# Opening the first layer of a two-layer decoder trunk from packed, feature-major inputs

## The chip, the cores and the metric

The kernel runs on one core of one Trainium2 chip. The metric is the device time of one execution in microseconds (us); before the change it is 2598.28 us, the median of three runs (2598.2 to 2599.01).

## What is computed

A trunk of two layers on 1024 tokens with 1024 features. Each layer normalises the tokens, projects them, runs two attention mixers (a dilated windowed one and a "stick-breaking" one), merges them through gates, adds the result to the residual stream `x`, and then runs a gated convolutional feed-forward part with 2816 channels. What matters here is the very beginning of layer 0:

```
def rmsnorm(x, g):
    y = x * rsqrt(mean(x * x, axis=-1) + 1e-6)
    return y * g

h = rmsnorm(x, norm1[l])
proj = h @ w_in[l]
qa, ka, va, qb, kb, vb, gate_pre = split(proj, ...)
z = qb @ kb.T / 8                        # stick-breaking scores, per head
later = reversed running sum of log(1 - sigmoid(z)) over earlier keys
o_b = exp(log(sigmoid(z)) + later) @ vb
```

A token's norm factor multiplies its whole row of `h`, so `vb` can be formed from `x * g` first and be multiplied by the token's factor afterwards.

## The kernel before

Activations stand feature-major on chip: 128 partitions hold features, the free dimension holds tokens, 8 feature chunks `k`, two token halves `n` of 512. Products on TensorE (PE) use float32 data split in two parts: `hi`, a rounded copy made by ScalarE (ACT), and `lo = x - hi`, made by VectorE (DVE). Each product is three matmuls (`product`, L187 to L189): hi by hi, hi by lo, lo by hi. So every operand costs one ACT and one DVE instruction on 128x512.

Layer 0 begins with `first` and `head`. `first` loads `x` token-major, eight tiles of 128 tokens (`xr`, L2023), squares each on ACT with an accumulated row sum (L2053), takes the root and reciprocal (L2056, L2057), and turns the tiles on PE (`x_t`, L2044; 64 transposes of `x` itself and 16 of the two tiles that are scaled before they are turned, `xsq`). ACT copies the turned tiles out of PSUM (`x_part`, L2073), from where they are stored to `xs` in DRAM for the residual stream, and DVE scales them with the gain and the factor (`h_raw`, L2090). `head` makes 256 value columns (`v_ps`, four banks of 48 matmuls of 256 columns), then keys and queries of the first two stick-breaking heads (`kq_ps`, `q_ps`, 24 matmuls of 512 columns for each of the two token halves). Part of the weight splitting and the rebuilding of `h_raw` for the first tokens runs on GpSimd (POOL; L175, L176, L2037, L2110).

Behind the opening comes the dense stage. It takes column pairs of `w_in` (`pair`, tile `in_a`) through a scheme of seven half-size products instead of eight (`seven`, L1058 to L1060, tiles `i_a`, `i_b`, `i_c`). The scheme needs sums of quarters of `h`: `block_sums` makes `h_sum` (L1081, L1086), rewrites `h_raw` in place (L1087, L1090), and splits the sums into `t_hi`, `t_lo`; and sums of quarters of the weights, L1186, L1189, L1193, each followed by a split into `w_hi`, `w_lo` (L145, L153). All of this is DVE and ACT work. Between these products stands the stick-breaking attention: scores `z` (L648, L649), sigmoids on ACT (`beta`, `stay`), a running product on DVE (L743), `beta * stay` on DVE (L750), and a transposition of that on PE (`sb_t`, L758).

PE's order is the program's order throughout. ACT and DVE run their queues in order too; what stands where in them is set by the program's order in the first steps (`manual_schedule`) and by the scheduler of the framework after that. All DMAs that matter are issued by SyncE (SP) in order, over eight semaphores in turn.

Of the kernel before, what the change touches and what calls it, by code (L numbers as in the profile page):

```python
# [34 lines left out]
WARM = 3  # L35
# [22 lines left out]
TWICE = 2  # L58
# [7 lines left out]
def trunk_kernel(ctx, tc, x, norm1, vecs, w_in, w_br, w_o, w_up, w_down, norm_f, out, depth=None, probe=None):  # L66
# [12 lines left out]
    make_identity(nc, ident)  # L79
    ones = cp.tile([P, 1], F32, name="ones")  # L80
    pool.memset(ones, 1.0)
    eps = cp.tile([P, 1], F32, name="eps")
    pool.memset(eps, EPS)
    zero = cp.tile([P, 1], F32, name="zero")
    pool.memset(zero, 0.0)
# [6 lines left out]
    def masks():  # L92

        t = [sb.tile([P, 256], F32, tag="pt", bufs=PT, name=f"msk{i}") for i in range(3)]
        pool.iota(t[1], [[-1, 256]], base=P, channel_multiplier=1, allow_small_or_imprecise_dtypes=True)
        pool.affine_select(t[1], t[1], [[-1, 256]], ALU.is_ge, FAR, base=P, channel_multiplier=1)
        pool.affine_select(t[2], t[1], [[1, 256]], ALU.is_ge, FAR, base=0, channel_multiplier=-1)
        dve.tensor_copy(base0, t[2])
        pool.memset(over, 0.0)
        pool.affine_select(over[:, HF - P : HF], over[:, HF - P : HF], [[-1, P]], ALU.is_gt, 1.0, base=0, channel_multiplier=1)  # L100
        rem = sb.tile([P, 256], I32, tag="pt", bufs=PT, name="rem")
        pool.iota(rem, [[-1, 256]], base=256, channel_multiplier=1)
        one = dve.tensor_scalar(rem, rem, 3, None, ALU.bitwise_and)
        tc.add_manual_dep(one.ins, LAST["g0"], NO_SYNC, reason="in turn")
        dve.tensor_copy(t[0], rem)
        dve.tensor_scalar(t[0], t[0], FAR, None, ALU.mult)
        LAST["base"] = dve.tensor_tensor(base2, t[1], t[0], ALU.add).ins.name

# [52 lines left out]
    def weights(src, cols, place=None, eng=None):  # L161
# [3 lines left out]
        src = src.rearrange("(k p) n -> p k n", p=P)  # L165
        for r in range(0, KD, per):
# [7 lines left out]
            if eng:  # L174
                eng.tensor_copy(hi, raw)  # L175
                LAST.setdefault("pools", []).append(pool.tensor_tensor(lo, raw, f32(hi), ALU.subtract).ins.name)  # L176
            else:
                split(hi, lo, raw)
# [286 lines left out]
    def x_in(n, h):  # L465

        if h == 0:
            X[n] = [None, None]
        X[n][h] = quarter(f"x{n}")
        nc.sync.dma_start(X[n][h], xs[n][:, 4 * h : 4 * h + 4, :])  # L470
# [137 lines left out]
    def kq_half(c, w, n):  # L608
        o = bank("ps", "kq_ps"[c:])
# [7 lines left out]
    def head(l, dense=None):  # L617


        def place(n, name):  # L620
            x = [big(name, F32R) for _ in range(n)]
            return ([x[0][:, h, :] for h in range(2)] if n == 1 else [y.rearrange("p a b -> p (a b)") for y in x])

        wv = weights(w_in[l][:, OFF_VB : OFF_VB + 256], 256, place(2, "v_w")) if l else early.pop("wv")
        others = lambda: [weights(w_in[l][:, off : off + P], P, place(1, "kq_w"), None if l else pool) for off in (OFF_KB, OFF_QB)]
        if l:
            wk, wq = others()
        yield
        vt = new_v("vb")
        if l:  # L630
            yield from values_part(vt, wv, range(2))
        else:
            yield from values_part(vt, wv, range(1))
            wk, wq = others()
            yield from values_part(vt, wv, range(1, 2))
        for n in range(2):
            yield from kq_half(0, wk, n)
            yield from kq_half(1, wq, n)
            if n == 0 and not l:
                one = table(AF.Sigmoid, zero[:, 0:1])  # L640
                tc.add_manual_dep(one.ins, LAST["head"][0], NO_SYNC, reason="behind")
                yield from values_part(vt, wv, range(2, 4))
                dense.done.add("wv")
        if l:
            yield from values_part(vt, wv, range(2, 4))
# [685 lines left out]
    def mixer(l, pending):  # L1331
# [19 lines left out]
        else:  # L1351
            first_units = relay(head(l, dense))

            with tc.manual_schedule(engines={ET.Activation, ET.DVE}):
                next(pending)
                next(first_units)
                for n in (1, 2):
                    next(pending)
                    for _ in range(n):
                        next(first_units)  # L1360
            for i, _ in enumerate(pending):
                for _ in range(2):
                    next(first_units, None)
                if i == 3:
                    dense.prime(1)
            for _ in first_units:
                dense.aside()
# [85 lines left out]
        for i, ab in order:  # L1453
            n, e = todo[i]
            sl = slice(n * HF, (n + 1) * HF)
            if i not in seen:
# [4 lines left out]
                if i in X_AT:  # L1461
                    late_x = X_AT.index(i)
                    x_in(late_x // 2, late_x % 2)
# [436 lines left out]
    heads, early = {}, {}  # L1900
# [109 lines left out]
    def first():  # L2010
        g_raw = sb.tile([KD, P], F32, tag="ot", name="g_raw")
        nc.scalar.dma_start(g_raw, norm1[0].rearrange("(c p) -> c p", p=P))
        gb = [bank("o", "gb") for _ in range(2)]
        warm = sb.tile([P, 8], F32, tag="ss", bufs=2, name="warm")
        act.activation(warm[:, 0:1], eps, AF.Sqrt)
        xr, rest, tps, parts, factor, raw_t, part = {}, {}, {}, {}, {}, {}, {}
        raw = big("w_raw").rearrange("p a (b c) -> p (a b) c", c=256)
        wv = early["wv"] = []

        def load(i):  # L2020
            if i < 8:
                xr[i] = sb.tile([P, T], F32, tag="p4", bufs=4, name="xr")
                nc.sync.dma_start(xr[i], xin[i * P : (i + 1) * P, :])  # L2023

        def weights_in(r):
            nc.sync.dma_start(raw[:, r : r + 2, :], w_in[0].rearrange("(k p) n -> p k n", p=P)[:, r : r + 2, OFF_VB : OFF_VB + 256])

        def weights_hi(r):
            hi = sb.tile([P, 2, 256], F32R, tag="wh", bufs=4, name="w_hi")
            lo = sb.tile([P, 2, 256], F32R, tag="wl", bufs=4, name="w_lo")  # L2030
            act.copy(hi, raw[:, r : r + 2, :])
            wv.extend((hi[:, i, :], lo[:, i, :]) for i in range(2))
            parts[r] = hi, lo

        def weights_lo(r, eng=dve):
            hi, lo = parts[r]
            one = eng.tensor_tensor(lo, raw[:, r : r + 2, :], f32(hi), ALU.subtract)  # L2037
            if eng is pool:
                LAST["pool"] = one.ins.name

        def turned(src, tag):
            got = [bank(tag, "x_t") for _ in range(2)]
            for k in range(KD):
                pe.transpose(got[k // 4][:, (k % 4) * P : (k % 4 + 1) * P], src[:, k * P : (k + 1) * P], ident)  # L2044
            return [tp.rearrange("p (e t) -> p e t", e=4) for tp in got]

        def scaled(i):
            if i in (0, 2):
                rest["pair"] = big("xsq")
            sq = rest[i] = rest["pair"][:, i % 2, :] if i < 4 else sb.tile([P, T], F32, tag="ot", name="xsq")  # L2050
            ss = factor[i] = sb.tile([P, 8], F32, tag="ss", bufs=2, name="ss")
            with tc.high_priority(offset=AHEAD):
                one = act.activation(sq, xr[i], AF.Square, accum_out=ss[:, 0:1])  # L2053
                if i >= TWICE + 2:
# [175 lines left out]
```

## Time and profile before

| | |
|---|---|
| median of three runs | 2598.28 us |
| the profiled execution | 2600.39 us, of which the span of its instructions is 2598.4 us |
| PE busy | 99% of the span, granted clock 0.999 |
| DVE, ACT, POOL busy | 80%, 52%, 4% |
| first product of `v_ps` | 9.12 us from the span's start |
| first product of the dense stage (`i_a`) | 65.02 us |
| first `sb_t` transposition | 82.63 us |

Times in rows are from the span's start. In a timeline row the first number is the start, the second the time from there to the end of the last instruction of the row; instructions of one kind that follow each other are one row (`x4`), and what ended a wait stands in brackets. Since instructions on one engine overlap a little, the distance of two starts is the price of one instruction; the time of a row with n of them, less one duration, over n-1 gives it too.

### The profile page before, as it was taken

The numbers are of one execution on the slowest core, as the hardware profiler recorded it, in microseconds if no ns is written. First come the engines' busy times: TensorE is split into PE (matmuls) and PEld (weight loads), VectorE is DVE, ScalarE is ACT, GpSimd is POOL, SyncE is SP. The second block draws the span as 40 slices with busy tenths as digits, with TensorE's granted clock in tenths as the row PEclk, the third lists the DMA queues.
The fourth block names the chain that finished last, engine by engine and source line by source line (L and its number), as shares of the span: only waits on it lengthen the run. The fifth ranks groups of instructions, "written<-read, shape, count | busy, mean of one in ns | idle before, by whom it ended". The sixth has DMA issues, their size and how long they took to land.

```text
span 2598.4 us, 35940 instructions
## 1 busy us (share of the span) xinstructions
PE 2585.0 (99%) x12600; PEld 2161.4 (83%) x12600; DVE 2088.0 (80%) x3482; ACT 1340.1 (52%) x2506; POOL 105.5 (4%) x145
## 2 busy tenths in 40 slices
PE   9999999999999999999999999999999999999999
PEld 8888888888888888888888888888888888888887
DVE  8878777795988888897678788777869888889966
ACT  6555666573554555422445565666645555544223
POOL 3000000030000000000000000000300000000000
PEclk9999999999999999999999999999999999999999
DMA  7534588973344444688444446798633344456963
GB/s 256 153 119 134 161 209 225 236 237 97 90 146 157 143 163 146 235 327 315 152 143 148 126 132 175 199 238 239 205 99 121 125 154 154 140 176 246 346 242 134
DMA packets 400772, 470.59 MB, mean 181 GB/s; under 512 B 24616, under 2 KB 315856, under 8 KB 398800
## 3 DMA queue, kind: packets, MB, share of 16 engines
q1 hardware_dynamic: 399728, 465.90, 56.1%
q0 software_dynamic: 704, 2.13, 0.4%
q8 instruction: 100, 1.64, 0.3%
q14 instruction: 80, 0.66, 0.1%
q10 hardware_dynamic: 160, 0.27, 0.0%
HBM read 305.59 MB, written 162.63 MB: 180 GB/s over the span
## 4 chain that ended last, share of the span: by engine, by line
PE 92%; DVE 4%; ACT 2%; DMA 1%; issue 1%; POOL 0%; DVEq 0%; ACTq 0%; POOLq 0%
PE u_a L1058 5%; PE u_a L1059 5%; PE u_a L1060 5%; PE d_ps L1818 5%; PE d_ps L1819 5%; PE d_ps L1820 5%; PE i_a L1058 5%; PE i_a L1059 5%; PE i_a L1060 5%; PE u_c L1058 3%; PE u_c L1059 3%; PE u_c L1060 3%; PE i_c L1058 2%; PE i_c L1060 2%; PE i_c L1059 2%; PE o_ps L188 2%
## 5 line engine op out<-in xcount | busy, mean ns | idle before, releaser
L145 ACT CAST w_hi<-up_a 128x512 fp32r<-128x512 f32 x280 | 173.9, 622 | 277.2 <-DVE up_a L1672 120.8
L153 DVE TENSOR_TENSOR w_lo<-up_a,w_hi 128x512 fp32r<-128x512 f32 x280 | 189.5, 689 | 83.5 <-ACT w_hi L145 83.5
L145 ACT CAST w_hi<-in_a 128x512 fp32r<-128x512 f32 x252 | 156.3, 622 | 161.6 <-PE i_c L1059 33.2
L153 DVE TENSOR_TENSOR w_lo<-in_a,w_hi 128x512 fp32r<-128x512 f32 x252 | 172.8, 688 | 72.6 <-ACT w_hi L145 60.6
L1829 DVE TENSOR_TENSOR x<-x,d_ps 128x512 f32<-128x512 f32 x220 | 150.2, 684 | 60.5 <-PE d_ps L1820 57.2
L1058 PE MATMUL u_a<-hh,w_hi 128*128 128x512 f32 x320 | 124.5, 389 | 0.0
L1060 PE MATMUL u_a<-hh,w_lo 128*128 128x512 f32 x320 | 124.5, 389 | 0.0
L1059 PE MATMUL u_a<-t_lo,w_hi 128*128 128x512 f32 x320 | 124.5, 389 | 0.0
L1060 PE MATMUL u_a<-t_hi,w_lo 128*128 128x512 f32 x320 | 124.5, 389 | 0.0
L1059 PE MATMUL u_a<-hl,w_hi 128*128 128x512 f32 x320 | 124.5, 389 | 0.0
L1058 PE MATMUL u_a<-t_hi,w_hi 128*128 128x512 f32 x320 | 124.5, 389 | 0.0
L1818 PE MATMUL d_ps<-gd_in,w_hi 128*128 128x512 f32 x316 | 123.2, 390 | 0.0
L1819 PE MATMUL d_ps<-gd_in,w_hi 128*128 128x512 f32 x316 | 123.0, 389 | 0.0
L1820 PE MATMUL d_ps<-gd_in,w_lo 128*128 128x512 f32 x316 | 123.0, 389 | 0.0
L1058 PE MATMUL i_a<-hh,w_hi 128*128 128x512 f32 x288 | 117.8, 409 | 0.0
L1058 PE MATMUL i_a<-t_hi,w_hi 128*128 128x512 f32 x288 | 116.5, 404 | 0.0
L1060 PE MATMUL i_a<-hh,w_lo 128*128 128x512 f32 x288 | 113.1, 393 | 0.0
L1060 PE MATMUL i_a<-t_hi,w_lo 128*128 128x512 f32 x288 | 113.0, 392 | 0.0
L1059 PE MATMUL i_a<-t_lo,w_hi 128*128 128x512 f32 x288 | 113.0, 392 | 0.0
L1059 PE MATMUL i_a<-hl,w_hi 128*128 128x512 f32 x288 | 112.9, 392 | 0.0
L1818 PE MATMUL d_ps<-gd_in,wd 128*128 128x512 f32 x284 | 110.9, 390 | 0.0
L1820 PE MATMUL d_ps<-gd_in,wd 128*128 128x512 f32 x284 | 110.5, 389 | 0.0
(403 smaller groups left out, 7723.4 us busy)
## 6 DMA issues: line engine op xcount, KB each, us to landing
gd<-g SPq DMA_DIRECT2D x154, 512.0 KB, 3.1
gd_in<-gd SPq DMA_DIRECT2D x154, 512.0 KB, 6.0
up_a<-in_w_up_dram SPq DMA_DIRECT2D x80, 512.0 KB, 5.4
in_a<-in_w_in_dram SPq DMA_DIRECT2D x72, 512.0 KB, 5.4
wd_raw<-in_w_down_dram SPq DMA_DIRECT2D x22, 1024.0 KB, 10.9
gin<-gs SPq DMA_DIRECT2D x32, 512.0 KB, 4.5
w_raw<-in_w_o_dram SPq DMA_DIRECT2D x64, 256.0 KB, 3.0
gs<-u SPq DMA_DIRECT2D x48, 256.0 KB, 3.2
```

The lines of the kernel that those rows point to most:

```text
L145: one = act.copy(hi, src)
L153: two = dve.tensor_tensor(lo, src, f32(hi), ALU.subtract)
L188: pe.matmul(o, lh, rl, start=False, stop=False, skip_group_check=share)
L1058: pe.matmul(o, w[0][:, c], rh, start=(first and i == 0), stop=False, skip_group_check=True)
L1059: pe.matmul(o, w[0][:, c], rl, start=False, stop=False, skip_group_check=True)
L1060: pe.matmul(o, w[1][:, c], rh, start=False, stop=(last and i == 3), skip_group_check=True)
L1818: pe.matmul(o, wh[:, c], gh, start=(i == 0 and k in (0, 4, 5)), stop=False, skip_group_check=True)
L1819: pe.matmul(o, wh[:, c], gl, start=False, stop=False, skip_group_check=True)
L1820: pe.matmul(o, wl[:, c], gh, start=False, stop=(i == m - 1), skip_group_check=True)
L1829: dve.tensor_tensor(x, x, o, ALU.add)
```

## The change

The host hands in three packed arrays more: `xt`, the transposed `x` in three blocks of tokens (0 to 255, 256 to 511, 512 to 1023); `wh`, the columns of `w_in` for values, keys and queries of the head, laid out by partition; and `gt0`, the first gain by partition. The opening becomes one function:

- `x` comes feature-major into the tiles `h_raw` by DMA, 256 tokens and two chunks at a time, alternating with value weights. The 80 transposes, the copies out of PSUM, the store to `xs` and all GpSimd work on weights and `h_raw` are gone.
- For tokens 0 to 511, ACT and DVE make `hi` and `lo` of `x * g` (L2040, L2044, 128x256 each), PE makes the value products from those, and the factor is applied when the bank is read out (L2139, L2137).
- The sums of squares come from ACT squares (L2048), DVE additions and 16 matmuls with a column of ones (L2085), followed by root, reciprocal and four transposes that spread the factors (`nrm_b`, L2119).
- DVE then multiplies `h_raw` in place by gain and factor (L2124), and ACT and DVE split it again (L2125, L2128), for keys and queries: chunk by chunk, PE following (L2148 to L2150). Key and query weights are split by ACT and DVE (L2104, L2108).
- The second 512 tokens are scaled likewise; their squares are taken token-major on ACT (L2178) from four tiles of `x` loaded beside. PE makes their values (L2058), then their keys and queries.
- The residual `x` is read from `xt` instead of `xs`; layer 1's head reads its weights from `wh`.

The core of the diff:

```diff
-            first_units = relay(head(l, dense))
-            with tc.manual_schedule(engines={ET.Activation, ET.DVE}):
-                next(pending)
-                next(first_units)
...
+            opening = first(dense)
+            with tc.manual_schedule(engines={ET.Activation, ET.DVE, ET.Pool}):
+                next(opening)
+            for _ in opening:
                 dense.aside()
...
+        def u_hi(k, t):
+            act.mul(H[0][0][:, k, t], RAW[0, k // 4][:, k % 4, t], g0[:, k : k + 1])
+        def u_lo(k, t):
+            hi, lo = (y[:, k, t] for y in H[0])
+            dve.scalar_tensor_tensor(lo, RAW[0, k // 4][:, k % 4, t], g0[:, k : k + 1], f32(hi), ALU.mult, ALU.subtract)
...
+        def scale(n, k, rb):
+            h_ = RAW[n, k // 4][:, k % 4, :]
+            dve.scalar_tensor_tensor(h_, h_, g0[:, k : k + 1], rb, ALU.mult, ALU.mult)
+            act.copy(H[n][0][:, k, :], h_)
+        def rest(n, k):
+            one = dve.tensor_tensor(H[n][1][:, k, :], RAW[n, k // 4][:, k % 4, :], f32(H[n][0][:, k, :]), ALU.subtract)
...
+        for k in range(KD):
+            if k + 1 < KD:
+                scale(0, k + 1, rb)
+            if k in (1, 2):
+                kq_hi(k - 1, 4)
+            rest(0, k)
+            if k in (1, 2):
+                kq_lo(k - 1, 4)
+            for c in range(2):
+                kq_step(c, k, o[c], 0)
+            if 2 <= k < 6:
+                act.activation(xr[k - 2], xr[k - 2], AF.Square, accum_out=ss[1][:, k - 2 : k - 1])
+            if k == 5:
+                roots(1, ss[1][:, 0:4])
+                table(AF.Sigmoid, ss[1][:, 0:1])
+            if k == 6:
+                factors(1)
+                rb1 = across(1)
```

What stands in the queues now, at three places.

PE at the start. Before, the transposes of the first scaled tile stand ahead of the first value product (`warm` are filling products, `gb` spreads the gain):

```order
L2117 MATMUL warm<-ident 128x128 x3
L2129 MATMUL warm<-ident,g_raw 128x8
L2133 MATMUL gb<-ident,g_81 128x128 x8
L2117 MATMUL warm<-ident 128x128 x4
L2044 MATMUL x_t<-ident,xsq 128x128 x8
L2117 MATMUL warm<-ident 128x128
L187 MATMUL v_ps<-w_hi,hh_190 128x256
```

Now, the end of the value products of tokens 256 to 511 and the step to the keys:

```order
L2058 MATMUL v_ps<-w_lo,hh_110 128x256 x4
L2085 MATMUL nrm_t<-ones,sq 128x1 x4
L2058 MATMUL v_ps<-w_hi,hh_110 128x256 x4
L2058 MATMUL v_ps<-w_hi,hl_111 128x256 x4
L2058 MATMUL v_ps<-w_lo,hh_110 128x256 x4
L2085 MATMUL nrm_t<-ones,sq 128x1 x12
L2119 MATMUL nrm_b<-ident,ss 128x128 x4
L2148 MATMUL kq_ps<-hh_110,kq_w 128x512
```

The value products now come in one row of 96 behind 18 filling products, and keys wait behind sums, root, factor and spreading.

ACT in the first half's keys and queries. Before, the table for the sigmoid is loaded once all of `hh` is made:

```order
L145 CAST hh_439<-h_raw 128x4x128 x2
L601 ACTIVATE kq_h<-q_ps 128x512
L493 ACT_TABLE_LOAD
L493 ACTIVATE junk<-zero,eps 128x1
L145 CAST t_hi<-h_sum 128x512 x4
```

Now the squares of the later tokens (`xr`), their root and the table load stand between the `hi` parts of chunks 4 to 7 (`hh`, L2125):

```order
L2178 ACTIVATE xr,ss<-xr 128x1024
L2125 CAST hh_110<-h_raw 128x512
L2178 ACTIVATE xr,ss<-xr 128x1024
L2125 CAST hh_110<-h_raw 128x512
L2178 ACTIVATE xr,ss<-xr 128x1024
L2111 ACTIVATE ss<-ss,eps 128x4
L497 ACT_TABLE_LOAD
L497 ACTIVATE junk<-ss,eps 128x1
L2125 CAST hh_110<-h_raw 128x512
```

The `hi` part of the last chunk has moved behind the table load.

DVE around the reading out of the second half's keys (`kq_l`, L605 before, L609 now). Before:

```order
L1086 TENSOR_TENSOR h_sum<-h_raw 128x512
L153 TENSOR_TENSOR w_lo<-in_a,w_hi 128x512
L1087 TENSOR_TENSOR h_raw<-h_raw,h_sum 128x512
L153 TENSOR_TENSOR t_lo<-h_raw,t_hi 128x512 x2
L1189 TENSOR_TENSOR in_a<-in_a 128x512
L605 TENSOR_TENSOR kq_l<-kq_ps,kq_h 128x512
L153 TENSOR_TENSOR t_lo<-h_raw,t_hi 128x512 x2
L153 TENSOR_TENSOR w_lo<-in_a,w_hi 128x512
L1193 TENSOR_TENSOR in_a<-in_a 128x512 x2
```

Now:

```order
L2128 TENSOR_TENSOR hl_473<-h_raw,hh_472 128x512 x2
L1073 TENSOR_TENSOR h_sum<-h_raw 128x512 x4
L150 TENSOR_TENSOR t_lo<-h_sum,t_hi 128x512
L2208 TENSOR_TENSOR vb<-v_ps,vb 128x4x2x64 x2
L150 TENSOR_TENSOR t_lo<-h_sum,t_hi 128x512
L609 TENSOR_TENSOR kq_l<-kq_ps,kq_h 128x512
L150 TENSOR_TENSOR t_lo<-h_sum,t_hi 128x512 x2
L150 TENSOR_TENSOR w_lo<-in_a,w_hi 128x512
L1078 TENSOR_TENSOR h_sum<-h_raw 128x512 x2
L1079 TENSOR_TENSOR h_raw<-h_raw,h_sum 128x512 x2
```

Four additions `h_sum`, four rewritings of `h_raw`, and splits of sums and weights that stood ahead of `kq_l` now stand behind it. From `kq_l` to the second `beta` (L750 before, L742 now) DVE's queue holds 31 instructions before and 50 now, both counts with two running products. PE's queue holds the same rows in the same order as before from the second half's keys to the end of the program; ACT's and DVE's do from a few dozen rows behind the second `beta`.

More of the change, by code (lines that the diff above doesn't have):

```diff
@@ L638, in head @@
             yield from kq_half(1, wq, n)
[L639 to L645, printed above, removed]
+        yield from values_part(vt, wv, range(2, 4))
     def scores(o, qt, ql, k):
@@ L2035, in weights_lo @@
[L2035 to L2045, printed above, removed]
@@ new lines, in total @@
+        def total(sq, c, first, last):
+            for a in range(2):
+                pe.matmul(tot[:, c : c + 1], sq[:, a, (c % 2) * P : (c % 2 + 1) * P], ones, start=(first and a == 0), stop=(last and a == 1), skip_group_check=True)
+        for q in range(4):
+            for k in (2 * q, 2 * q + 1):
+                u_hi(k, late)
+                u_lo(k, late)
+            sqs[1, q] = square(q, late)
+            v_step([1], q, [o2])
+            if q < 2:
+                dve.tensor_tensor(sqs[0, 0], sqs[0, 0], sqs[0, 2 + q], ALU.add)
+            if q == 2:
+                dve.tensor_tensor(sqs[1, 0], sqs[1, 0], sqs[1, 1], ALU.add)
+                for c in range(2):
+                    total(sqs[0, 0], c, True, True)
@@ L2219 @@
     arrays, args = {}, []
-    inputs = {**inputs, "vecs": vectors(inputs)}
+    inputs = {**inputs, "vecs": vectors(inputs), **packed(inputs)}
     for name in _INS:
```

385 lines of the change are left out of this document (200 added, 185 removed).

## The prediction

> **What bounds the kernel now.** The page's first part comes first, then busy time by stretch, then the timelines of PE and DVE where DVE is full. Columns of the second: stretch, length, PE busy, PEld, DVE, ACT, POOL (instructions), granted clock, DMA share, GB/s.
>
> ```profile
> PE 2585.0 (99%) x12600; PEld 2161.4 (83%) x12600; DVE 2088.0 (80%) x3482; ACT 1340.1 (52%) x2506; POOL 105.5 (4%) x145
> ```
>
> ```profile
> 5.00:29.60 24.60, 23.60 (x180) 22.21 (x178) 19.17 (x48) 21.84 (x47) 14.31 (x15) 1.00 0.92 303
> 29.60:42.60 13.00, 13.00 (x70) 10.97 (x67) 12.84 (x36) 8.77 (x17) 4.33 (x5) 1.00 0.88 276
> 42.60:54.10 11.50, 11.50 (x97) 11.50 (x96) 10.30 (x18) 5.46 (x9) 0.00 (x0) 1.00 0.66 220
> 54.10:65.00 10.90, 10.90 (x50) 9.03 (x49) 8.78 (x15) 5.02 (x9) 0.00 (x0) 1.00 0.57 196
> 65.00:80.00 15.00, 15.00 (x68) 12.33 (x67) 13.81 (x22) 12.04 (x24) 0.72 (x2) 1.00 0.47 141
> 80.00:100.00 20.00, 20.00 (x102) 16.22 (x101) 19.91 (x31) 12.76 (x27) 0.58 (x2) 1.00 0.61 197
> 100.00:150.00 50.00, 49.97 (x253) 41.48 (x252) 35.19 (x57) 26.50 (x55) 2.99 (x7) 1.00 0.40 120
> ```
>
> PE is never idle from 29.6 us to 100 us, and 0.03 us in the next 50. Time that PE saves or loses early reaches the end, unless a later wait takes it back. But DVE is busy for 19.91 of the 20 us from 80: it has nothing to give there. So I look at what PE takes from DVE at that place.
>
> ```profile
> 54.11 0.40 PE L187 MATMUL kq_ps<-hh,kq_w 128*128 128x512 f32 x1
> 59.58 0.39 PE L187 MATMUL q_ps<-hh,kq_w 128*128 128x512 f32 x1
> 65.02 0.39 PE L1058 MATMUL i_a<-hh,w_hi 128*128 128x512 f32 x1
> 82.63 0.59 PE L758 MATMUL sb_t<-ident,beta 128*128 128x128 f32 x3
> ```
>
> ```profile
> 60.40 0.69 DVE L605 TENSOR_TENSOR kq_l<-kq_ps,kq_h 128x512 fp32r<-128x512 f32 x1 [1.17 <-ACT kq_h L604]
> 64.91 0.69 DVE L153 TENSOR_TENSOR w_lo<-in_a,w_hi 128x512 fp32r<-128x512 f32 x1 [0.69 <-ACT w_hi L145]
> 65.90 0.69 DVE L602 SCALAR_TENSOR_TENSOR kq_l<-q_ps,kq_h 128x512 fp32r<-128x512 f32 x1 [0.30 <-ACT kq_h L601]
> 76.15 0.69 DVE L1222 TENSOR_TENSOR u<-u,i_c 128x512 f32<-128x512 f32 x1 [0.54 <-issue]
> 77.67 1.22 DVE L743 TENSOR_TENSOR_SCAN stay<-stay,over 128x512 f32<-128x512 f32 x1 [0.23 <-ACT stay L724]
> 80.34 1.21 DVE L743 TENSOR_TENSOR_SCAN stay<-stay,over 128x512 f32<-128x512 f32 x1
> 82.05 0.68 DVE L750 TENSOR_TENSOR beta<-beta,stay 128x512 f32<-128x512 f32 x1
> ```
>
> The last of these, the second `beta`, ends at 82.73; PE transposes `beta` from 82.63, the first three from the earlier one. DVE is just in time, with no slack. Between the first `kq_l` and this `beta` it waited only 0.69 + 0.30 + 0.54 + 0.23 = 1.76 us. So two clocks count: when PE reaches the dense stage (65.02), and when DVE has worked off its queue (82.73). The later one sets the end.
>
> **The opening on PE, up to the keys.** These rows price it:
>
> ```profile
> 0.81 0.20 POOL masks.py:197 MEMSET ident<- 128x128 f32 x1 [0.29 <-POOLq L2218]
> ```
>
> ```profile
> 1.81 1.65 PE L2117 MATMUL warm<-ident 128*128 128x128 f32 x6 [1.81 <-POOL ident masks.py:199]
> 5.67 1.92 PE L2117 MATMUL warm<-ident 128*128 128x128 f32 x8
> 28.69 1.04 PE L2044 MATMUL x_t<-ident,xr 128*128 128x128 f32 x8
> 42.60 0.28 PE L187 MATMUL v_ps<-w_hi,hh 128*128 128x256 f32 x1
> 629.36 0.95 PE L538 MATMUL nrm_t<-ones,nrm 128*128 128x1 f32 x8
> ```
>
> ```profile
> 630.34 0.26 ACT L540 ACTIVATE ss<-nrm_t,eps 128x4 f32<-128x4 f32 x1 [0.35 <-PE nrm_t L538]
> ```
>
> ```profile
> 630.64 0.18 DVE L541 RECIPROCAL ss<-ss 128x4 f32<-128x4 f32 x1
> ```
>
> The filling products need one memset, done at 1.0; 18 at 0.24 to 0.275 are 4.4, until 5.4. The value products of tokens 256 to 511 took 54.11 - 42.60 = 11.5 for 96, so 0.12 each: until 16.9. Sixteen column sums at 0.12 make 18.8, and one wait for the last quarter's `w_lo` some 0.4: 19.2. Then the new chain: root 0.26, reciprocal 0.18, four spreading transposes at most 0.6 (0.13 each in the `x_t` row), the first scaling 0.74, the first `hi` 0.62 and hand-overs of 0.25 in all. The first key product starts at about 21.9, and DVE's first scaling at 20.6.
>
> Do data and splits keep up? The weights' first 512 KB loads land in
>
> ```profile
> DMA to landing us min/median/max: 4.1/5.4/6.8
> ```
>
> and the windows show 303 GB/s, so 2 MB of early `x` and values need 7 us beyond the first landing near 4.7; PE wants its last quarter at 14. ACT has 16 `hi` parts of 128x256 in this stage, for which the nearest rows are
>
> ```profile
> L671 ACT COPY fold<-sb_o 64x256 f32<-64x256 f32 x32 | 11.8, 369 | 20.7 <-PE sb_o L664 16.3 <-DMA sq<-last 2.1 <-ACT u L1211 1.9
> L812 ACT ACTIVATE p<-p,st 128x256 f32<-128x256 f32 x56 | 28.0, 501 | 2.8 <-DVE st L811 2.8
> ```
>
> 0.37 to 0.50 each, with splits and squares 11 to 12.6 us, less than PE's 13.8. This work lies beside PE; if the cover goes, by later data, PE waits the difference. The removed transposes, copies and GpSimd work are what makes the first product of keys start at 21.9 and not 29.6: 7.7 us early.
>
> **Keys, queries and the second half: DVE.** Its prices:
>
> ```profile
> L555 DVE SCALAR_TENSOR_TENSOR h_raw<-x,vec,nrm_b 128x512 f32<-128x512 f32 x16 | 11.2, 742 | 2.8 <-PE nrm_b L547 2.8
> ```
>
> ```profile
> L153 DVE TENSOR_TENSOR hl<-h_raw,hh 128x512 fp32r<-128x512 f32 x12 | 10.0, 844 | 0.3
> L153 DVE TENSOR_TENSOR w_lo<-in_a,w_hi 128x512 fp32r<-128x512 f32 x4 | 2.8, 688 | 0.7 <-ACT w_hi L145 0.7
> ```
>
> ```profile
> 45.61 2.50 DVE L153 TENSOR_TENSOR t_lo<-h_sum,t_hi 128x512 fp32r<-128x512 f32 x4
> ```
>
> Four splits in 2.50 with one at 0.69 give (2.50 - 0.69)/3 = 0.603 as the price of each; scaling, 0.742 less the same overlap of 0.08, costs 0.66. The 844 ns of `hl` fall in the stretch in which POOL works, 688 without it. I take 0.603 throughout, since POOL has only constants left; were 844 ns to hold for the 16 `hl` of the two halves, they would cost 16 x 0.156 = 2.5 us more, and this goes into the range. The Trainium skill, "SBUF — State Buffer", section "Who interferes with whom", says that a DVE instruction with two SBUF inputs and a GpSimd instruction that reads SBUF hold each other up; the two rows agree with it, and by it the 12 x 0.156 = 1.9 us that `hl` lost before go with GpSimd's splitting, as in my sum.
>
> First half: 8 scalings and 8 `lo` parts and 3 `kq_lo` are 5.3 + 4.8 + 1.8 = 11.9 us on DVE, against 48 products at 5.47/24 = 0.228, or 10.9, on PE. DVE is the longer, and it waits besides:
>
> ```profile
> 4.66 1.06 ACT L2053 ACTIVATE xsq<-xr 128x1024 f32<-128x1024 f32 x1 [1.73 <-DMA xr<-in_x_dram]
> 5.62 0.19 ACT L2053 ACTIVATION_READ_ACCUMULATOR xsq<-xr 128x1 f32 x1
> 43.47 1.28 ACT L493 ACT_TABLE_LOAD   x1
> 44.77 0.30 ACT L493 ACTIVATE junk<-zero,eps 128x1 f32<-128x1 f32 x1
> 59.78 0.59 ACT L604 CAST kq_h<-kq_ps 128x512 fp32r<-128x512 f32 x1 [2.38 <-PE kq_ps L189]
> ```
>
> ACT has a square (1.06 + 0.19), the root (0.26), the table (1.28) and the dummy (0.3) ahead of the last `hi`: 3.1 us in which DVE has nothing else in its queue, and behind it the whole second half waits. Two `kq_lo` wait for `kq_hi`, queued behind a `hi`: about 0.7 each. So the last `lo` is done at 20.6 + 11.9 + 1.4 + 3.1 = 37.0.
>
> Second half: 8 x 0.66 + 8 x 0.603 + 4 reads of 128x256 at 0.39 (no row has one; 0.33 to 0.66 bounds it) + 0.6 + 0.66 = 13.0, with two waits of 0.65 again 14.3: `lo` of the last chunk at 51.3. The last 16 value products make 53.2, 24 key products 58.7, and ACT's read 0.59 with a hand-over lets DVE's first `kq_l` start at **59.6** (60.40 before). The dense stage follows 5.47 behind the keys, at **64.1** (65.02). Of the 7.7 us PE keeps 0.9.
>
> **The queue behind `kq_l`.** Four sums, four rewritings and splits have moved behind `kq_l`: its way to the second `beta` holds 50 instructions, two of them running products (1.14 by their row less the overlap), against 31. That is 48 x 0.603 + 2 x 1.14 + 0.08 = 31.3, with 0.3 of waits 31.6. `beta` ends at 59.6 + 31.6 = **91.2**, against 82.73: +8.5. The same sum for before, 29 x 0.603 + 2.3 + 1.76 + 0.08 = 21.6, falls 0.7 short of the measured 22.33, so +9.2 is as near; ends of the unknown prices give +6 to +12. PE's rows from the keys on are unchanged, so it stands still at `sb_t` for the whole, after a dense stage that began 0.9 early. Behind it PE is the bound as before and DVE has 15 us of idle in 100 to 150, but none of the lost PE time is given back.
>
> At nothing: the residual read from `xt` (PE waits for no residual in the rows above), packed weights of layer 1, the second `in_a` load behind more loads on SP. If that load's cover (PE's products of the first pair) is gone, 1.4 us, the slowest landing above less the median.
>
> Profiled, before is 2600.39 us (2598.4 of span and 1.99 around it), 2.1 above the median. 2600.39 + 8.5 = 2608.9 against that; as a difference on the median, 2598.28 + 8.5 = **2606.8 us**.
>
> **Rivals.**
> - **DVE waits nowhere** in both halves (the `hi` parts run far enough ahead). 20.6 + 11.9 + 13.0 = 45.5, + 1.9 + 5.47 + 0.8 gives `kq_l` at 53.7, `beta` at 85.3: +2.6, 2600.9. For it: ACT is at half load (5.02 of 10.9). Against: the queue order, which puts the table ahead of the last `hi`. Chance 0.12.
> - **Faster: PE leads.** PE alone needs 21.9 + 10.9 + 0.5 + 11.5 + 5.5 = 50.3 to the end of the keys, the dense stage 55.8, 9.2 early: 2589.1. But from its first scaling at 20.6 to the second `beta` DVE has 11.9 + 13.0 + 8 x 0.603 (the sums and splits between the last `lo` and `kq_l`) + 31.3 = 61.0 us of instructions without any wait, and would have to be through them by 82.73 - 9.2 = 73.5, in 53 us. It decides from 82.7 - 20.6 = 62.1: only if DVE's work and all its waits together stay below this is the kernel faster at all, and for the whole gain DVE's prices must fall by 13%. The rows above give 0.66 to 0.69 for one shape wherever POOL is still, and waits of 5.8 us more are forced by ACT's queue. Chance 0.04.
> - **Later data or a slower PE** ahead of `sb_t`: the four `x` tiles and the second `in_a` come late, or the clock drops in the wait. The slowest of the loads above lands 2.7 us behind the fastest; one such on the path gives 2609.5, two in a row 2612.2. The windows show clock 1.00 throughout and no such wait. The Trainium skill, "TensorE: Matmul & The Clock Gate", Part 1, says PE falls to half clock after some 3.4 us idle, which by an estimate from that page would add up to 1.7 us; no trace of before shows such an idle stretch. Chance 0.13.
>
> **How the numbers follow.** The forecast has 0.71, with 2604 to 2610 as its own range. With the third rival the range 2602 to 2612.5 holds a bit over 8 in 10. This kernel's runs tell 0.2%, 5.2 us, from no change: above 2603.5 counts as slower. Forecast less its low tail (0.01) and the third rival give slower 0.83; the first rival and the tail 0.13; faster 0.04.
>
> **What would show it.** First key product near 22; ACT's table load between two `hi`, PE waiting there for `hl` of DVE; `kq_l` of the second half at 59.6 and `i_a` at 64.1; DVE full from 50 to 95; second `beta` and PE's wait at 91. If `i_a` comes at 56, PE leads and I am wrong; if `i_a` is early and `beta` on time, the queue count is wrong.

## The result, and the profile after

The changed kernel takes 2662.82 us (median of four runs, 2661.26 to 2664.27) against 2598.27: a ratio of 1.0248, with a 95% interval from 1.023 to 1.0265. The forecast was 2606.8. The sign was right and the size was not: 64.6 us were lost and not 8.5. The profiled execution took 2662.97 us with a span of 2661.1, so what follows accounts for 2661.1 - 2598.4 = 62.7 us.

The page's first part, for the changed kernel:

```profile
PE 2634.5 (99%) x12565; PEld 2160.6 (81%) x12565; DVE 2097.8 (79%) x3467; ACT 1341.0 (50%) x2506; POOL 90.2 (3%) x128
```

PE is busy for 2634.5 us where it was busy for 2585.0, with 35 records fewer. So most of the loss is not waiting: PE works longer on the same products. A table by stretch shows where, first of the changed kernel, then of the kernel before (columns as in the prediction; the number behind PE's time counts its products).

```profile
22.00:29.00 7.00, 4.89 (x16) 3.36 (x16) 4.19 (x8) 3.14 (x6) 0.00 (x0) 0.51 0.42 170
...
80.00:90.00 10.00, 7.19 (x23) 5.36 (x24) 6.71 (x12) 5.77 (x12) 0.46 (x1) 0.83 0.25 68
90.00:100.00 10.00, 5.92 (x24) 3.94 (x24) 9.47 (x15) 5.37 (x13) 1.49 (x2) 0.86 0.35 112
100.00:105.00 5.00, 5.00 (x18) 3.90 (x16) 4.35 (x7) 1.72 (x3) 0.00 (x0) 0.59 0.18 66
```

```profile
800.00:1000.00 200.00, 200.00 (x860) 161.33 (x859) 164.66 (x243) 101.00 (x160) 0.00 (x0) 1.00 0.45 149
2000.00:2200.00 200.00, 200.00 (x866) 161.13 (x865) 168.40 (x261) 101.68 (x165) 0.00 (x0) 1.00 0.41 136
```

```profile
800.00:1000.00 200.00, 200.00 (x884) 165.68 (x883) 167.15 (x246) 102.04 (x161) 0.00 (x0) 1.00 0.46 155
2000.00:2200.00 200.00, 199.74 (x882) 165.06 (x881) 167.81 (x247) 104.23 (x166) 0.00 (x0) 1.00 0.44 150
```

Far behind the opening, in a feed-forward stage that the change does not touch, PE is busy for all of 200 us at full granted clock in both kernels. Yet it gets through 860 products instead of 884. Each costs 200/860 = 0.2326 us instead of 0.2262. The timeline shows the beat; before, and after (other products of `u_a` of the same shape, since the stage comes some 30 us later):

```profile
900.13 0.39 PE L1058 MATMUL u_a<-hh,w_hi 128*128 128x512 f32 x1
900.36 0.39 PE L1059 MATMUL u_a<-hl,w_hi 128*128 128x512 f32 x1
900.58 0.39 PE L1060 MATMUL u_a<-hh,w_lo 128*128 128x512 f32 x1
900.81 0.39 PE L1058 MATMUL u_a<-hh,w_hi 128*128 128x512 f32 x1
```

```profile
900.15 0.39 PE L1050 MATMUL u_a<-t_hi,w_hi 128*128 128x512 f32 x1
900.38 0.40 PE L1051 MATMUL u_a<-t_lo,w_hi 128*128 128x512 f32 x1
900.62 0.39 PE L1052 MATMUL u_a<-t_hi,w_lo 128*128 128x512 f32 x1
900.85 0.40 PE L1050 MATMUL u_a<-t_hi,w_hi 128*128 128x512 f32 x1
```

Three products take 0.68 us before and 0.70 after. That is the larger part. The smaller one is the opening, PE first and DVE below it:

```profile
1.07 6.21 PE L2035 MATMUL warm<-blank 128*128 128x128 f32 x36 [1.07 <-POOL eps L88]
7.03 0.72 PE L2058 MATMUL v_ps<-w_hi,hh 128*128 128x256 f32 x4
...
19.74 2.87 PE L2085 MATMUL nrm_t<-ones,sq 128*128 128x1 f32 x24
...
25.84 0.80 PE L2148 MATMUL kq_ps<-hh,kq_w 128*128 128x512 f32 x1 [1.55 <-ACT hh L2125]
...
68.34 0.40 PE L1050 MATMUL i_a<-hh,w_hi 128*128 128x512 f32 x1
...
82.74 0.50 PE L1050 MATMUL i_c<-hh,w_hi 128*128 128x512 f32 x1 [3.93 <-ACT w_hi L142]
```

```profile
98.83 1.20 PE L750 MATMUL sb_t<-ident,beta 128*128 128x128 f32 x3 [3.98 <-DVE beta L742]
```

```profile
24.33 0.75 DVE L2124 SCALAR_TENSOR_TENSOR h_raw<-h_raw,g,nrm_b 128x512 f32<-128x512 f32 x1 [1.21 <-PE nrm_b L2119]
...
40.19 0.69 DVE L2128 TENSOR_TENSOR hl<-h_raw,hh 128x512 fp32r<-128x512 f32 x1 [1.94 <-ACT hh L2125]
...
63.56 0.69 DVE L609 TENSOR_TENSOR kq_l<-kq_ps,kq_h 128x512 fp32r<-128x512 f32 x1 [3.41 <-ACT kq_h L608]
...
82.20 1.90 DVE L150 TENSOR_TENSOR w_lo<-in_a,w_hi 128x512 fp32r<-128x512 f32 x3 [2.06 <-ACT w_hi L142]
...
98.02 1.26 DVE L742 TENSOR_TENSOR beta<-beta,stay 128x512 f32<-128x512 f32 x2
```

The wait of 3.93 us for `w_hi` goes back to the load of the second column pair, `in_a`. ACT, which makes `w_hi`, waits for it; SP issues it at 76.93, and at 64.93 before:

```profile
81.55 2.18 ACT L142 CAST w_hi<-in_a 128x512 fp32r<-128x512 f32 x4 [2.08 <-DMA in_a<-in_w_in_dram]
```

```profile
76.93 1.06 SPq L1164 DMA_DIRECT2D in_a<-in_w_in_dram  x2
```

```profile
64.93 0.58 SPq L1172 DMA_DIRECT2D in_a<-in_w_in_dram  x1
```

The first `sb_t` starts at 98.83 instead of 82.63: 16.2 us are lost by then, at the wait for the second `beta`, where the loss was forecast. The other 62.7 - 16.2 = 46.5 us come behind it, where the forecast had nothing. Right behind it PE runs at half clock until about 104 us (0.59 in the five us from 100). Past that, the 300th of the 10056 products of 512 columns, which come in one order in both kernels from the 49th on, starts at 118.48 us before and at 137.61 after. So some 19.1 us belong to the opening and 43.5 to the rest of the program.

### The profile page after: what moved, and what is told of

It is laid out like the page before. It is cut to its first block, busy times and chain, and to the rows that moved or that the text cites. A ratio compares the mean times of both kernels' runs of the same rounds, so it can differ in the third digit from the quotient of the medians.

```text
span 2661.1 us, 35816 instructions
## 1 busy us (share of the span) xinstructions
PE 2634.5 (99%) x12565; PEld 2160.6 (81%) x12565; DVE 2097.8 (79%) x3467; ACT 1341.0 (50%) x2506; POOL 90.2 (3%) x128
## 3 DMA queue, kind: packets, MB, share of 16 engines
q0 software_dynamic: 704, 2.13, 0.3%
q8 instruction: 99, 1.62, 0.3%
## 4 chain that ended last, share of the span: by engine, by line
PE 93%; DVE 3%; ACT 2%; DMA 1%; issue 1%; SPq 0%; DVEq 0%; ACTq 0%
PE u_a L1052 6%; PE u_a L1051 6%; PE u_a L1050 6%; PE d_ps L1799 5%; PE d_ps L1801 5%; PE d_ps L1800 5%; PE i_a L1050 4%; PE i_a L1051 4%; PE i_a L1052 4%; PE u_c L1052 3%; PE u_c L1050 3%; PE u_c L1051 3%; PE o_ps L180 2%; PE o_ps L181 2%; PE o_ps L182 2%; PE i_c L1052 2%
```

## The experiments

Two questions were open: what slows PE for the rest of the kernel, and what the loss in the opening is made of.

**Where the tiles stand.** Behind the opening the products, their order and the clock are the same, but the change moves something else: the places of the tiles. A tile gets its place in the on-chip memory when it is first asked for. The new opening asks in another order, and among the large tiles lie small ones of 32 bytes a partition (`warm` and `ss`, `junk`). These are the addresses in the compiled programs, in bytes within a partition:

| tile | before | after |
|---|---|---|
| `hh` of the first half (moving operand) | 102688 | 98528 |
| `t_hi`, `t_lo`, the lowest of them (moving) | 8480 | 16608 |
| `hh` of the second half (moving) | 192800 | 184640 |
| `w_hi`, the first of four (stationary) | 86304 | 168224 |

Before, all of them leave 32 when divided by 128 (by 256 too). After, they leave 96, 96, 64 and 32 by 128. Over the whole program 9096 of the 10056 products of 512 columns have their operands at different addresses modulo 128 after the change, and none had before. Theory A is that this costs PE time. Rival B is that the half clock of the opening (0.51 in the rows above) leaves PE in a slower beat.

**e1: small tiles made wide.**

```diff
-        ss = sb.tile([P, 8], F32, tag="ss", bufs=2, name="ss")
+        ss = sb.tile([P, 32], F32, tag="ss", bufs=2, name="ss")
...
-        junk = sb.tile([P, 1], F32, tag="junk", name="junk")
+        junk = sb.tile([P, 32], F32, tag="junk", name="junk")[:, 0:1]
```

> The changed kernel with three small tiles (two of 32 bytes a partition, one of 4 in a 32-byte place) made 128 bytes wide, so that every tile starts at the same address modulo 128 bytes; the instructions stay. Theory A: a product of 512 columns costs about 5.4 ns more (233.1 against 227.7) where its moving and its stationary operand stand at different addresses modulo 128; 9096 of the 10056 such products do so in the changed kernel, none in the kernel before. It expects 2662.8 - 9096 x 5.4 ns = 2613.7, between 2603 and 2618, and the pitch of u_a back at 226.7 ns. Rival B: the pace was set by the half-clock stretches of the opening and stays; it expects 2662 again.

Measured: 2634.73 us (2633.7 to 2635.73), 28 us less than the changed kernel and 21 more than expected. Rival B falls: it expected 2662 again, and the half clock at 22 us is still there. But theory A gives too much.

**e2 and e3: the kernel before with an unused tile.**

```diff
     def new_h(n):
+        if n == 0 and H[0][0] is None:
+            sb.tile([P, 16], F32, tag="pad", name="pad")
```

(16 numbers in e2, 32 in e3.)

> The kernel before with an unused tile of 64 bytes a partition ahead of hh of the first half, nothing else. All tiles behind it move by 64 bytes, so 6504 of the 10056 products of 512 columns get operands at different addresses modulo 128. Theory A expects 2598.3 + 6504 x 5.4 ns = 2633.4, up to 2641 if each costs 6.6 ns. Rival B (half-clock stretches of the opening set the pace) expects 2598.

> The same with a tile of 128 bytes: all tiles behind it move, but no address modulo 128 changes. Theory A expects 2598.3, within 2 us. A rival by which any move of the tiles matters (distance in another unit, or the place itself) expects 2630 or so, as with 64 bytes.

Measured: e2 2613.18 us (ratio 1.005, interval 1.0035 to 1.0065), e3 2631.86 (1.0124, 1.0109 to 1.0139), with 2599.11 for the kernel before. An unused tile of 128 bytes costs 33 us. So places do matter, but theory A misses both: e2 costs 14 us and not 35, and e3 should have cost nothing. Modulo 128 is the wrong unit. The trace of e3 shows the culprits side by side, in groups of products of one stretch (800 to 1000 us; the columns at the end are busy time and mean ns of one):

```profile
L1061 PE MATMUL u_a<-t_lo,w_hi 128*128 128x512 f32 x86 | 33.5, 390 | 0.0
L1060 PE MATMUL u_a<-t_hi,w_hi 128*128 128x512 f32 x86 | 33.5, 389 | 0.0
...
L1060 PE MATMUL u_a<-hh,w_hi 128*128 128x512 f32 x80 | 31.6, 395 | 0.0
L1061 PE MATMUL u_a<-hl,w_hi 128*128 128x512 f32 x80 | 31.6, 395 | 0.0
```

In one trace and with the same weights the `t` products, whose tiles stayed where they were, take 389 to 390 ns, and the `hh` and `hl` products, whose tiles moved by 128 bytes, 395. (As before, a product's own time overlaps the next; the distance of starts differs by about as much.) I then took from the traces of before, after and e1 to e4 all distances between the starts of neighbouring products of 512 columns that are below 260 ns, and sorted them by the address of the moving operand less that of the stationary one:

| difference modulo 256 | 0 | 32 | 64 | 96 | 128 | 192 |
|---|---|---|---|---|---|---|
| products | 29403 | 2500 | 6069 | 560 | 12313 | 5411 |
| mean distance, ns | 228.1 | 232.9 | 229.7 | 233.7 | 232.7 | 233.0 |

Sorting by larger moduli separates hardly more, by smaller ones much less. So theory A': the unit is 256 bytes. e1 has 3312 products left at 128. By its own mean distances the changed kernel would take 9372 products x (232.57 - 227.67) ns = 45.9 us more than before, near the 43.5 us above.

**e5 and e6: everything at one address modulo 256.**

```diff
-        junk = sb.tile([P, 32], F32, tag="junk", name="junk")[:, 0:1]
+        junk = sb.tile([P, 64], F32, tag="junk", name="junk")[:, 0:1]
```

(e5, on e1; e6 is e3 with 64 numbers.)

> e1 with the 128 byte tile of the table load made 256 bytes wide. The rows of e1, e2 and e3 say that the unit is not 128 but 256 bytes: with operands at the same address modulo 256 a product of 512 columns starts 228.1 ns after the one before on the mean, at a difference of 128 bytes 232.7. e1 has left 3312 products at a difference of 128, this kernel none. Theory A': 2634.7 - 3312 x 4.6 ns = 2619.5. The rival (e1 already has what the places can give, and the rest is the opening) expects 2634.7.

> The kernel before with an unused tile of 256 bytes a partition at the place of e2 and e3. Theory A' (address difference modulo 256): no product changes, so 2599.1 as the kernel before, within 2 us. A rival by which the distance itself or the end of the memory matters expects more than e3's 2631.9, or a value between.

Measured: e5 2619.24 us (1.0073, 1.0056 to 1.0089), e6 2599.53 (1.0, 0.9991 to 1.0009). Both are where theory A' has them, within 0.5 us, which is closer than their own runs lie together (3.35 and 2.05 us). e5 is the change without its accident of places, 43.6 us below the changed kernel, and in the stretch from 800 us it makes 884 products again, at 2000 us 883:

```profile
800.00:1000.00 200.00, 200.00 (x884) 165.69 (x883) 167.81 (x247) 101.38 (x160) 0.00 (x0) 1.00 0.47 154
2000.00:2200.00 200.00, 200.00 (x883) 165.40 (x882) 170.83 (x258) 104.89 (x169) 0.00 (x0) 1.00 0.44 145
```

What is left, 2619.24 - 2599.61 = 19.6 us, belongs to the opening: e5 is already 18.8 us late at the 300th product.

**e4: the second `in_a` sooner.** It stands on e1, so at the places of e1:

```diff
         for c in range(2):
-            one = nc.sync.dma_start(
...
+            with tc.high_priority(offset=SOON):
+                one = nc.sync.dma_start(
...
```

> e1 with the loads of in_a given a higher priority, so that the second pair's load stands 12 rows earlier in SP's queue, ahead of most loads of kv and slots. In the changed kernel PE waited 3.93 us for w_hi of that pair and ran at half clock behind it. If this wait lies on the path, the time is 3.9 + 1.6 us below e1: about 2608. If DVE's queue to the second beta is the bound (the prediction's step), it stays at e1's 2614 within 1.5 us.

Measured: 2629.49 us, 5.24 less than e1 (5.5 expected). The late load lay on the path, and through DVE: with it early the queue from `kq_l` to the second `beta` runs without that gap.

```profile
63.65 0.69 DVE L610 TENSOR_TENSOR kq_l<-kq_ps,kq_h 128x512 fp32r<-128x512 f32 x1 [3.41 <-ACT kq_h L609]
...
93.85 1.26 DVE L743 TENSOR_TENSOR beta<-beta,stay 128x512 f32<-128x512 f32 x2
```

From 63.65 to 93.85 + 1.26 = 95.11 are 31.5 us for 50 instructions; the prediction had 31.6.

**e7 and e8: less DVE work and waiting in the opening.** Both stand on e5 and e4 together. e7 moves work into the wait for the first factor (the same lines leave the loop over the chunks), e8 also shortens the sums.

```diff
+        for r in (0, 4):
+            for c in range(2):
+                kq_hi(c, r)
+                kq_lo(c, r)
+        for i in range(4):
+            act.activation(xr[i], xr[i], AF.Square, accum_out=ss[1][:, i : i + 1])
         roots(0, tot[:, 0:4])
         factors(0)
...
+        roots(1, ss[1][:, 0:4])
+        table(AF.Sigmoid, ss[1][:, 0:1])
```

```diff
-        for i, q in enumerate((0, 2, 3)):
-            for c in (2, 3):
-                total(sqs[1, q], c, i == 0 and c == 2, i == 2)
+        dve.tensor_tensor(sqs[1, 2], sqs[1, 2], sqs[1, 3], ALU.add)
+        dve.tensor_tensor(sqs[1, 0], sqs[1, 0], sqs[1, 2], ALU.add)
+        for c in (2, 3):
+            total(sqs[1, 0], c, True, True)
```

(The second is e8's.)

> e5 and e4 together, and the opening's ACT and DVE work in another order: all splits of key and query weights, the four squares, both roots and the table load stand ahead of the first scaling, in the 4.3 us in which ACT and DVE wait for the first factor. Without the new order e5 and e4 together would be 2629.5 - 15.2 = 2614.3. If DVE's queue to the second beta is the bound, 4 x 0.6 us of splits and waits of 0.66 + 0.66 + 1.94 us leave it: the second beta comes 5.5 us sooner and the time is about 2608.8. If the bound is elsewhere (PE, loads), it stays within 1.5 us of 2614.3.

> e7 with two DVE additions more in the first stage and 8 column sums instead of 16 on PE; each sum takes two records of 0.12 us, so the first factor should come 1.9 us sooner. If the chain from the sums to the second beta sets the end, 1.9 us less than e7, about 2606.9; if DVE has other work to wait for ahead of kq_l, no change.

Measured: e7 2608.24 us (1.0033, 1.002 to 1.0046), 0.6 below what the DVE theory gave and 6 below its rival. (The 2614.3 from which both start is a sum; e5 and e4 together, without the new order, were not run.) e8 2610.99 (1.0044, 1.0029 to 1.0059), no gain: a miss. Both wait for the factor until the same time, as PE's rows of e7 and then e8 show; below them are ACT's rows of e8:

```profile
24.38 1.11 PE L2121 MATMUL nrm_b<-ident,ss 128*128 128x128 f32 x4 [1.29 <-DVE ss L2116]
26.99 0.80 PE L2150 MATMUL kq_ps<-hh,kq_w 128*128 128x512 f32 x1 [1.49 <-ACT hh L2127]
```

```profile
24.33 1.11 PE L2122 MATMUL nrm_b<-ident,ss 128*128 128x128 f32 x4 [3.28 <-DVE ss L2117]
```

```profile
22.79 1.04 ACT L2166 ACTIVATE xr<-xr 128x1024 f32<-128x1024 f32 x1
...
23.82 0.24 ACT L2114 ACTIVATE ss<-nrm_t,eps 128x4 f32<-128x4 f32 x1
```

The sums were done sooner, but ACT's root stands behind four squares, which ACT works through from 19.66 on without a wait until it comes to the root at 23.82. What PE saved became 3.28 us of waiting instead of 1.29. Why e8 is 2.7 us above e7 is not settled.

**e9 to e12: is there a version that beats both?** e9 stands on e8: it puts one square ahead of the root, one behind it and two into the loop, adds 10 filling products around the factor and takes 5 from the start, and issues the block sums two at a time. e10 is e9 without the filling products around the factor. e11 is e9 with a higher priority for DVE's running products. e12 is e9 with eight block sums on GpSimd, and it reads out the first half's keys and queries one scaling earlier.

```diff
             for _ in opening:
-                dense.aside()
+                for _ in range(ASIDES):
+                    dense.aside()
...
+        far_square(0)
         roots(0, tot[:, 0:4])
         factors(0)
-        kq_hi(1, 0)
+        far_square(1)
+        fill(FILL[0])
         rb = across(0)
+        fill(FILL[1])
```

```diff
-                if c1 == L:
-                    one = dve.tensor_tensor_scan(rev, rev, over[:, HF - (c1 - c0) : HF][:, ::-1], 1.0, ALU.mult, ALU.max)
+                with tc.high_priority(offset=AHEAD):
+                    if c1 == L:
+                        one = dve.tensor_tensor_scan(rev, rev, over[:, HF - (c1 - c0) : HF][:, ::-1], 1.0, ALU.mult, ALU.max)
...
```

```diff
+            if l == 0:
+                pool.tensor_tensor(b21(i), b21(i), b11(i), ALU.subtract)
+                return
             behind(dve.tensor_tensor(b21(i), b21(i), b11(i), ALU.subtract))
```

(The first is e9's, the second e11's, the third one of the two of e12. `fill` issues filling products; `ASIDES` is 2, `FILL` is (3, 7) in e9 and (0, 0) in e10.)

> e8 with three edits: only one of the four squares stands ahead of the first root (in e8 the root waited for the last of them, so the shorter sums gave nothing), 10 filling products stand around the spreading of the factor and 13 instead of 18 at the start, and the block sums are issued two at a time, so that between kq_l and the second beta DVE has 41 instructions instead of 50. By the DVE theory: factor 2.6 us sooner, 3.3 us of DVE's idle time ahead of kq_l filled, and 2.9 us saved if PE keeps its full clock in the keys' stage (in e7 it ran at half from 22.5 to 32.7): the second beta at about 83 to 84 and 2600, between 2598 and 2604. A rival by which PE, not DVE, is now the bound of the opening expects 2604 to 2608.

> e9 without the 10 filling products around the factor. If idle time on PE is what brings the half clock at 22 us, it comes back here, and keys cost up to 2.9 us more: 2602.5 to 2603. If the clock falls anyway, or DVE is the bound of this stage, the same as e9 within 1 us.

> e9 with a higher priority for the running products, so that 36 instead of 41 instructions stand from kq_l to the second beta. If PE still waits for that beta, 5 x 0.6 = 3 us less than e9, down to what PE alone needs; if it does not wait there any more, the same within 1 us.

Measured: e9 2603.15 us (1.0016, 1.0006 to 1.0025), near the dear end of its range. In its trace PE keeps its full clock from 22 to 33 us, where e7 has 0.53, and DVE is still what PE waits for at `sb_t`:

```profile
22.00:33.00 11.00, 11.00 (x61) 9.04 (x61) 10.17 (x18) 7.66 (x16) 0.00 (x0) 1.00 0.29 117
```

```profile
86.01 0.30 PE L753 MATMUL sb_t<-ident,beta 128*128 128x128 f32 x1 [2.98 <-DVE beta L745]
```

e10 took 2606.82 (1.0033, 1.002 to 1.0046), 3.7 more than e9, and not for the reason expected: its clock from 22 to 33 us is 1.00 as well, so the filling products around the factor are not what keeps it. Idle time alone is not what takes it away either. In the changed kernel the clock falls while PE is still busy with a row of column sums, as its windows show (clock 1.00, then 0.66):

```profile
21.00:22.00 1.00, 1.00 (x11) 1.00 (x11) 0.00 (x0) 0.00 (x0) 0.00 (x0) 1.00 1.04 430
22.00:22.60 0.60, 0.60 (x5) 0.52 (x4) 0.00 (x0) 0.00 (x0) 0.00 (x0) 0.66 1.03 423
```

(Each sum leaves two records, and 24 of them stand in one row of 2.87 us above.) In e7 it falls during the same 24 records (0.76 from 22 to 23 us), in e8 in the wait of 3.28 us (0.78 from 22 to 23.5). e9 and e10 have at most 8 such records in a row and no wait above 1.54 us there. That a long row of one-column products counts like idle time fits all five, but no run tests it alone.

The first `sb_t` of e10 comes even sooner than e9's, 84.39 against 86.01. Around 1895 us its products are level with e9's (0.2 us later), and by 2084 us they are 3.7 us later: in between PE waits 2.13 us for `u` ahead of `u_c` at 2011 us and runs at half clock behind it. This is one execution, 1.9 us above e10's median; what causes the wait is open.

e11 took 2609.33 (1.004, 1.0025 to 1.0055), 6.2 more than e9: a miss that says something. Its rows on PE:

```profile
83.08 0.44 PE L754 MATMUL sb_t<-ident,beta 128*128 128x128 f32 x2 [0.29 <-DVE beta L746]
```

```profile
93.00 0.79 PE L1055 MATMUL i_a<-hl,w_hi 128*128 128x512 f32 x1 [5.35 <-DVE hl L153]
```

The wait for `beta` is down to 0.29 us, and a wait of 5.35 us for `hl` stands 10 us behind it: the instructions that `beta` overtook are late instead. This fits DVE's work as a whole being what binds, and not its order.

> e9 with eight of the block sums' additions on GpSimd (which stands still there) and the reading out of the first half's keys and queries one scaling earlier. From kq_l to the second beta DVE then has 36 instructions instead of 41, so 3.0 us less, and 1.15 us of waits for kq_h go; 8 additions of 1.3 us on GpSimd may slow some 16 of DVE's by 0.156 us each, 2.5 us at most. If DVE's queue is still the bound (in e9 PE waits 2.98 us for that beta): 2603.2 less 1.7 to 4.2, about 2600, level with the kernel before. If contention takes it all back: 2603. Below 2597.5 it would beat both kernels.

Measured: 2602.36 us (1.0012, 1.0003 to 1.0021), at the dear end of what was expected. GpSimd's additions take 1.62 us each and not 1.3, and DVE's instructions beside them are slowed; rows of POOL, then of DVE:

```profile
L1077 POOL TENSOR_TENSOR h_sum<-h_raw 128x512 f32<-128x512 f32 x4 | 6.4, 1623 | 30.9 <-DVE h_raw L2136 30.9
```

```profile
61.06 3.31 POOL L1089 TENSOR_TENSOR h_raw<-h_raw 128x512 f32<-128x512 f32 x2 [3.93 <-DVE h_raw L1085]
```

```profile
61.43 1.78 DVE L1084 TENSOR_TENSOR h_sum<-h_raw 128x512 f32<-128x512 f32 x1
63.14 1.77 DVE L153 TENSOR_TENSOR w_lo<-in_a,w_hi 128x512 fp32r<-128x512 f32 x1
64.84 0.68 DVE L1085 TENSOR_TENSOR h_raw<-h_raw,h_sum 128x512 f32<-128x512 f32 x1
```

1.77 us instead of 0.68: an instruction that meets one of GpSimd's may wait it out, 1.1 us and not the 0.156 that the mean of `hl` before suggested. The Trainium skill, "SBUF — State Buffer", section "Who interferes with whom", says of such pairs that one holds the other up; the trace agrees.

In e12 PE waits only 0.2 us for `beta`. In its place stands a wait for `w_hi`, whose sum of weights comes late in DVE's queue, and half clock behind it (0.51 from 71 to 74.4 us):

```profile
70.94 0.71 PE L1053 MATMUL i_a<-t_hi,w_hi 128*128 128x512 f32 x1 [2.29 <-ACT w_hi L145]
```

e9 and e12 come within 0.2% of the kernel before. None beats it.

## Why the prediction was wrong

**The step that failed** is the last of the queue part: "PE's rows from the keys on are unchanged, so it stands still at `sb_t` for the whole". The rows are unchanged, but not their price. 0.228 us for a product of 512 columns was read from the trace of before and carried over as if it belonged to the instruction. It belongs to the instruction and the addresses of its operands. I compared the order of instructions on each engine and never the places of the tiles, which the change moves for the whole program. This was 43.6 of the 64.6 us by the medians: e5, which moves tiles and changes nothing else, gives 2662.82 - 2619.24 back. e3 and e6, which move tiles in the kernel before, show the same cause without the change. No rival had it. And e5's 2619.24 lies above the top of the range, 2612.5, too, so the opening was short as well.

**The opening** was right in its mechanism and short in two terms, the start of the first scaling and the second `in_a`. DVE's queue to the second `beta` sets the end, as forecast, with 16.2 us instead of 8.5:

- The first scaling starts at 24.33, not 20.6. Filling ends at 7.03 instead of 5.4, and the column sums take 32 records of 0.12 us where I had counted 16: the row `nrm_t` ... x8 that I read covers four sums, each of which leaves two records. 1.6 + 1.9 = 3.5 us of the 3.7. The filling products were misread in the same way: the 18 leave 36 records, while the row of 6 from which I took 0.275 us apiece holds three products.
- The first half took DVE from 24.33 to 40.19 + 0.69 = 40.88: 16.5 us, forecast 16.4, with the wait for the last `hi` behind the table load. e7 took this load and the `kq_lo` splits away from there and gained as the sum said.
- `kq_l` starts at 63.56 instead of 59.6, nearly all of it (3.7 of 4.0 us) carried over from the start. The dense stage starts at 68.34 and not 64.1.
- The queue behind it took 31.5 us where nothing disturbs it (e4), forecast 31.6. In the changed kernel it takes 98.02 + 1.26 - 63.56 = 35.7, since the second `in_a` is late. I had put that at nothing, 1.4 us if its cover went; PE waited 3.93, and e4 shows 5.2 us for it. It was part of the third rival.
- The half clock, also in that rival, came three times: the rows above show 0.51, 0.83 and 0.86 of full clock in 7, 10 and 10 us, and the third stretch goes on behind `sb_t` (0.59). The Trainium skill, "TensorE: Matmul & The Clock Gate", Part 1, gives about 3.4 us of idleness as what halves the clock. The traces agree for the waits of 3.93 and 3.98 us, but the clock also fell behind shorter ones: 2.98 us in e9 (0.57 from 87 to 91 us), 2.29 in e12 (0.51 from 71 to 74.4) and 2.13 in e10 (0.57 from 2012 to 2016). The waits of 0.72 and 1.54 us in e10 did not lower it.

e5 leaves 19.6 us to the opening, 3.4 more than the 16.2 at `sb_t`. The half clock behind `sb_t`, from 98.83 to about 104.1, accounts for half of these 5.3 us, 2.6; the rest is within what the runs vary.

The second rival, faster, asked whether DVE is through with its work and its waits by 82.73. No version got there: the second `beta` ends at 86.47 in e9, 85.45 in e12, and 83.03 in e11, where other work was late for it. e9 and e12 come to the level of the kernel before and not below. They still contain waits of 2.98 and 2.29 us on PE, both behind DVE's queue; that no order of its work could do better is not shown.

## What to carry to other kernels

A change that asks for tiles in another order, or adds a tile of a few bytes, moves all that stand behind it. Compare the addresses of the operands of the costly products before and after, and not the order of instructions alone; here it was enough to give the small tiles sizes that put all operands at one address modulo 256 (128 bytes for `warm` and `ss`, 256 for `junk`). When PE's busy time grows with its number of instructions unchanged, take the distance of starts in a stretch that the change does not touch: it tells a price from a wait in one row. Ask how many records one product leaves before a row is divided by its count. And where a queue is full up to a deadline, its length is what counts: in e11, moving some instructions forward made others late.

## What the runs showed of the hardware

- A product of 512 columns follows the one before after 228.1 ns on the mean if its moving and stationary operands stand at the same address modulo 256 bytes, and after 229.7 to 233.7 at differences of 32 to 192. The granted clock is 1.00 in the stretches from 800 and 2000 us of both kinds. Products of 256 columns showed no such difference that could be told from their scatter (114 to 120 ns in the median). Whether it is the stationary operand of the product itself or of the next one, loaded meanwhile, these runs don't tell apart.
- With the operands at one address modulo 256, the place itself made no difference to this distance: e5 has all of them at 224 modulo 256, before and e6 at 32, and the mean of the distances below 260 ns is 227.6 to 227.7 ns in all three.
- A column sum and a filling product leave two records each in these traces (16 and 18 products, 32 and 36 records), a transposition one (80 and 80).
- An unused tile of 128 bytes made this kernel 1.24% slower (1.0109 to 1.0139), one of 256 bytes did nothing (0.9991 to 1.0009).
